# A hybrid attention layer on one core: TensorE's order in the attention stages written out as a fixed software pipeline

## The chip, the cores and the metric

The kernel runs on one core of a Trainium2 chip. The metric is the device time of one execution in microseconds (us), as the median of several runs. A trace of one further, profiled execution is there for reading: the busy spans of the engines, their waits, and the transfers.

## The reference

One layer of a decoder works on one sequence of 2048 tokens with 1024 channels, all in float32. Eight heads of width 64 use forgetting attention (FoX), eight others stick-breaking attention; all are causal.

```python
h = rms_norm(x, g_attn) * (1.0 + scale_a) + shift_a     # shift, scale, gate: silu(c) @ w_ada + b_ada
q_f, k_f, v_f, q_s, k_s, v_s, f_logit = split(h @ w_in)
# FoX:            F = cumsum(log_sigmoid(f_logit + b));  softmax(q.k / 8 + F[t] - F[s]) over s <= t, times v
# stick-breaking: A[t,s] = sigmoid(z_ts) * prod_{s<j<t} (1 - sigmoid(z_tj)) over s < t, times v;  z = q.k / 8
x = x + gate_a * (concat(head_rms_norm(o_fox), head_rms_norm(o_sb)) @ w_out)
h = rms_norm(x, g_mlp) * (1.0 + scale_m) + shift_m
u = causal_depthwise_conv(h @ w_up)                      # width 3
x = x + gate_m * ((silu(u_gate) * u_val) @ w_down)
return rms_norm(x, g_final)
```

## The kernel before, in words

**Units.** Attention is cut into 32 units, `("sb" or "fox", p, tb)`: a kind, one of four pairs of heads, and one of four blocks of 512 queries. All stick-breaking units come first, then all FoX units; within a kind the pairs follow each other, and within a pair the blocks. A unit has a projection and an attention.

**The projection** (`proj`, `finish_proj`, `accumulate`; `norm_proj` for the first pair, which also normalises x) makes Q, K and V of the unit's 512 tokens. Each operand is held as a float32r number and its remainder (`split`: ScalarE copies, VectorE or GpSimd subtracts), so every product takes three matmuls. The normalised input lies in DRAM as eight tiles of 0.5 MB (`hs`), which come back through SyncE into ten `hp` buffers. Q takes 24 matmuls of 512 columns, K the same, both into `ps_pj` banks; V is made in even pairs only, for two pairs at once, by 96 matmuls of 256 columns, and read back from DRAM in odd pairs. Q and K pass through DMAs to be laid out (`Q<-q` L293, `K<-q` L303). Q has two buffers, K five, V six.

**The attention** of a unit (`attend`) goes through four head blocks: two blocks of 256 queries by two heads. A head block's keys come in chunks of 512.

- In stick-breaking (`sb_head`), for each chunk, from the last to the first, and each of two 128-query rows: logits (two matmuls, L378 and L379, into one of two `ps_qk` banks); two sigmoids on ScalarE (`rw`, `a`, L415 and L416); a scan on VectorE that multiplies from right to left (L424, L427); a product on GpSimd that yields the weights `a` (L431).
- In FoX (`fox_head`), for each row and all its chunks: logits, on VectorE the sum with the bias `Fb` and a running minimum (L460), and one exponential of the row on ScalarE (`p`, L464).
- Then both kinds go through `weighted`, once per 256 keys: four transposes of 128 x 128 on TensorE into one of three `ps_pt` banks (L388), a copy on ScalarE (L392) and a subtraction on VectorE (L393) into one of three `at` buffers, and four matmuls with V that add into the only `ps_pv` bank (L397). I call one such call a group. A unit has 6, 14, 22 or 30 groups for tb = 0 to 3, a pair 72.

When a head block's groups are done, ScalarE and VectorE read `ps_pv` out (L518, L519) into `oT`; after two heads `head_var` squares it on GpSimd and puts off a small matmul (L497) by 13 ticks.

**What sets the order.** The program is traced in an order: `interleave` runs the attention of a unit and pulls, in proportion, the steps of the next unit's projection and, in FoX, of `late_mod` (the other modulation vectors). But that is a priority only. A scheduler with a timing model of its own places the instructions of every engine, and it may take a later matmul ahead of an earlier one that has to wait. Each engine then runs the fixed sequence that results.

**Places named below.** `forget_sums` (L229) turns the forget-gate logits into the cumulated sums F: transfers, three activations, a transfer, four scans. It runs at unit ("sb", 1, 0). From unit ("sb", 0, 3) on, `long_rows` keeps a whole row in one `rw` buffer (4 of them). Pools are closed and opened at ("sb", 0, 3) and ("fox", 0, 0). After the last unit come `first_out`, the output projection, the MLP and the final norm.

Of the kernel before, what the change touches and what calls it, by code (L numbers as in the profile page):

```python
# [8 lines left out]
F32 = mybir.dt.float32  # L9
# [7 lines left out]
P = 128  # L17
# [16 lines left out]
def kernel(ctx: ExitStack, tc: tile.TileContext, x, c, w_ada, b_ada, g_attn, w_in, b_fgate,  # L34
# [96 lines left out]
    def interleave(main, n, fillers):  # L131
        live = [[g, k, 0] for g, k, _ in fillers if g is not None]
        for i, _ in enumerate(main):
            tick()
            for e in live:
                while e[2] < (i + 1) * e[1] / n:
                    e[2] += 1
                    if next(e[0], StopIteration) is StopIteration:
                        e[2] = 1 << 30
        for g, _, whole in fillers:  # L140
            if g is not None and whole:
                drain(g)

# [85 lines left out]
    def forget_sums():  # L229
        z = sx.tile([NTB * NH, TB], F32, name="fz", tag="a", bufs=8)  # L230
        e = sx.tile([NTB * NH, TB], F32, name="fe", tag="a", bufs=8)
# [9 lines left out]
        for t in range(NTB):  # L241
            e = sx.tile([NH, TB], F32, name="fl", tag="a", bufs=8)
            z = sx.tile([NH, TB], F32, name="fc", tag="a", bufs=8)
# [39 lines left out]
    def finish_proj(kind, p, tb, aq, w, hts, res, ak=None):  # L283
        Q = sb.tile([P, 2, 2, TB], F32R, name="Q", bufs=2)
        K = sb.tile([P, 2, TB], F32R, name="K", bufs=5)
# [22 lines left out]
        else:  # L308
            V1 = sb.tile([P, 4, 2, P], F32R, name="V", bufs=6)
# [72 lines left out]
    def weighted(o, kts, blk, V, hl, first, last, diag):  # L382
        b = pt()
        at = sb.tile([P, 2, 2 * 2 * P], F32R, name="at", bufs=3)
        order = [(1, 0), (0, 0), (0, 1), (1, 1)]
        for i, (kk, qi) in enumerate(order):
            if not (diag and i == 0):
                nc.tensor.transpose(b[:, i * P:(i + 1) * P], blk(kts[kk], qi), ident)  # L388
        lo = P if diag else 0
        if diag:  # L390
            nc.gpsimd.memset(f(at[:, :, 0:P]), 0.0)
        nc.scalar.activation(at[:, 0, lo:], b[:, lo:], AF.Copy)  # L392
        nc.vector.tensor_sub(at[:, 1, lo:], b[:, lo:], f(at[:, 0, lo:]))  # L393
        for kk, kt in enumerate(kts):
            for w in range(2):
                rhs = at[:, w].rearrange("p (s q) -> p s q", q=P)[:, 0:4:3, :] if kk else at[:, w, P:3 * P]
                nc.tensor.matmul(o[:, 0:2 * P], V[kt // 4][:, kt % 4, hl, :], rhs,  # L397
                                 start=first and kk == 0 and w == 0, stop=last and kk == 1 and w == 1)

    def sb_head(j, qc, hl, Q, K, V, o):  # L400
        n = (2 * j + 2 + 3) // 4
        right = [None, None]
        whole = [sx.tile([P, S + 1], F32, name="rw", bufs=4) for _ in range(2)] if long_rows else None
        for ch in range(n - 1, -1, -1):
            last = ch == n - 1
            at = []
            for qi in range(2):
                need = min(512, (2 * j + qi + 1) * P - ch * 512)
                b = logits(max(need, 2 * P), slice((qc + qi) * P, (qc + qi + 1) * P), hl, Q, K[ch])
                if long_rows:  # L410
                    r = whole[qi][:, ch * 512:ch * 512 + need + 1]
                else:
                    r = sx.tile([P, 512 + 1], F32, name="r", bufs=7)
# [3 lines left out]
                if last:  # L417
                    nc.gpsimd.memset(r[:, need:need + 1], 0.0)
                elif not long_rows:
                    nc.gpsimd.tensor_copy(r[:, need:need + 1], right[qi][:, 0:1])  # L420
# [618 lines left out]
```

## Time and profile before

| what | value |
|---|---|
| median of 3 runs | 3159.3 us (3159.17 to 3167.24) |
| the profiled execution | 3161.0 us |
| its span, first to last instruction | 3159.2 us |
| TensorE, VectorE, ScalarE, GpSimd busy | 94%, 67%, 52%, 42% of the span |
| granted TensorE clock, mean | 0.982 |
| first logits / first FoX transposes / last weighted sum of attention | 70.8 / 932.6 / 1621.0 us from the start of the span |

The page gives shares of busy time; the stage rows give the same for stretches that I chose. A matmul's recorded time contains its latency, and matmuls overlap, so a run of them is read by the time between its first start and last end. A wait is put down to the instruction that released it last.

### The profile page before, as it was taken

The page shows a single profiled execution, that of the slowest core. Times are in us where ns is not written, and L with a number is a line of the kernel's source. Part 1 is how long each engine was busy: PE and PEld are TensorE (multiplying, and loading weights), DVE is VectorE, ACT ScalarE, POOL GpSimd, SP SyncE. Part 2 cuts the span into 40 slices and gives each one's busy share as a digit, 9 for nine tenths or more (in the row PEclk, how much of TensorE's full clock was granted, in tenths as well). Part 3 has the DMA queues.
Part 4 walks back from the last instruction along what each step waited for, and adds up shares of the span by engine and source line. Part 5 has one row for each costly group of instructions (what it writes and reads, how often), then busy time and mean ns, then how long its engine had stood idle before and what let it go on. Part 6 is the DMA issues. An engine that isn't in the chain of part 4 may idle for free. (4 is left out here: it accounts for less than half of the span.)

```text
span 3159.2 us, 46407 instructions
## 1 busy us (share of the span) xinstructions
PE 2964.1 (94%) x15934; PEld 2510.7 (79%) x15934; DVE 2129.2 (67%) x3422; ACT 1650.8 (52%) x3033; POOL 1316.8 (42%) x1459
## 2 busy tenths in 40 slices
PE   6889798998989999999999989999899998999998
PEld 5778597987878789888877778888678887888887
DVE  6776689877876776556843587777987776244353
ACT  5664667766766565566743444444444443343332
POOL 2673666657553242242212344444444442322321
PEclk8999899999999999999999999999999999999999
DMA  9547432565346695685547632222222223554552
GB/s 266 185 128 272 136 112 87 165 212 158 128 129 211 203 304 194 171 308 162 170 130 228 214 104 81 87 83 86 88 74 86 84 89 115 197 203 154 192 200 90
DMA packets 292940, 496.51 MB, mean 157 GB/s; under 512 B 29448, under 2 KB 177664, under 8 KB 291680
## 3 DMA queue, kind: packets, MB, share of 16 engines
q1 hardware_dynamic: 281072, 480.92, 47.9%
q10 hardware_dynamic: 11632, 12.63, 1.1%
q8 instruction: 126, 2.06, 0.3%
q14 instruction: 110, 0.90, 0.1%
HBM read 352.61 MB, written 90.51 MB: 140 GB/s over the span
## 5 line engine op out<-in xcount | busy, mean ns | idle before, releaser
L828 PE MATMUL ps_o<-oa,wu 128*128 128x512 f32 x2088 | 503.1, 392 | 13.2 <-DVE oa L45 8.2
L828 PEld LDWEIGHTS ps_o<-oa,wu 128*128 128x128 f32 x2088 | 390.7, 188 | 104.0 <-DVE oa L45 12.4
L393 DVE TENSOR_TENSOR at<-ps_pt,at 128x512 fp32r<-128x512 f32 (+1 forms) x576 | 361.9, 650 | 127.2 <-ACT at L392 125.0
L281 PE MATMUL ps_pj<-hp,w_qk 128*128 128x512 f32 x1512 | 415.5, 408 | 29.6 <-DMA hp<-hs 10.0
L397 PE MATMUL ps_pv<-at,V 128*128 128x256 f32 x2304 | 415.5, 297 | 26.4 <-ACT at L392 11.9
L392 ACT ACTIVATE at<-ps_pt 128x512 fp32r<-128x512 f32 (+1 forms) x576 | 313.5, 577 | 210.6 <-PE ps_pt L388 165.2
L431 POOL TENSOR_TENSOR a<-a,rw 128x512 f32<-128x512 f32 (+2 forms) x272 | 332.3, 1237 | 208.3 <-DVE rw L427 82.8
L397 PEld LDWEIGHTS ps_pv<-at,V 128*128 128x128 f32 x2304 | 333.6, 191 | 64.0 <-DVE at L393 20.6
L281 PEld LDWEIGHTS ps_pj<-hp,w_qk 128*128 128x128 f32 x1512 | 280.7, 194 | 87.3 <-DMA hp<-hs 12.4
L45 DVE TENSOR_TENSOR wd<-wdraw,wd 128x1024 fp32r<-128x1024 f32 x88 | 113.1, 1285 | 260.9 <-ACT wd L44 260.9
L45 POOL TENSOR_TENSOR g<-graw,g 128x512 fp32r<-128x512 f32 x84 | 142.8, 1702 | 325.1 <-ACT g L44 324.2
L378 PE MATMUL ps_qk<-K,Q 128*128 128x512 f32 (+2 forms) x640 | 260.8, 409 | 15.3 <-ACT a L416 5.0
L978 PE MATMUL ps_o<-wd,g 128*128 128x512 f32 x1040 | 250.5, 391 | 8.7 <-ACT g L44 8.7
L427 DVE TENSOR_TENSOR_SCAN rw<-rw 128x512 f32<-128x512 f32 x168 | 242.1, 1460 | 19.0 <-ACT rw L415 18.5
L828 PE MATMUL ps_t<-ob,wu 128*128 128x512 f32 x984 | 241.5, 390 | 0.0
L320 PE MATMUL ps_pj<-w_v,hp 128*128 128x256 f32 (+1 forms) x1536 | 235.0, 290 | 5.5 <-DVE zn L326 2.5
L978 PEld LDWEIGHTS ps_o<-wd,g 128*128 128x128 f32 x1040 | 196.1, 189 | 49.9 <-ACT g L44 9.1
L379 PE MATMUL ps_qk<-K,Q 128*128 128x512 f32 (+2 forms) x640 | 235.1, 369 | 0.0
L44 ACT ACTIVATE wu<-wuraw 128x512 fp32r<-128x512 f32 x214 | 133.0, 626 | 189.0 <-PE ps_o L828 123.1
L388 PE MATMUL ps_pt<-edge,a 128*128 128x128 f32 x1088 | 186.2, 279 | 42.9 <-POOL a L431 40.1
L320 PEld LDWEIGHTS ps_pj<-w_v,hp 128*128 128x128 f32 x1536 | 210.3, 191 | 15.3 <-issue 3.1
L828 PEld LDWEIGHTS ps_t<-ob,wu 128*128 128x128 f32 x984 | 184.9, 188 | 38.9 <-ACT hf_m L733 0.3
(222 smaller groups left out, 5737.9 us busy)
## 6 DMA issues: line engine op xcount, KB each, us to landing
hp<-hs SPq DMA_DIRECT2D x224, 512.0 KB
wuraw<-in_w_up_dram SPq DMA_DIRECT2D x84, 512.0 KB
wdraw<-in_w_down_dram SPq DMA_DIRECT2D x84, 512.0 KB
Q<-q SPq DMA_DIRECT2D x128, 256.0 KB
g<-u SPq DMA_DIRECT2D x42, 512.0 KB
graw<-g SPq DMA_DIRECT2D x84, 256.0 KB
hs<-hp SPq DMA_DIRECT2D x32, 512.0 KB
K<-q SPq DMA_DIRECT2D x128, 128.0 KB
```

The costliest lines, as they stand in the source:

```text
L45: (lo_engine or nc.gpsimd).tensor_sub(lo, src, f(hi))
L281: nc.tensor.matmul(acc, w[kt][:, a, n], h[:, bb], start=kt == 0 and i == 0, stop=kt == KT - 1 and i == 2)
L320: nc.tensor.matmul(av[:, t * width:(t + 1) * width], hts[kt][:, a, tok], w[1][kt][:, bb, 0:width], start=kt == 0 and m == 0, stop=kt == KT ...
L378: nc.tensor.matmul(b[:, :cw], Q[:, hl, 0, qcols], K[:, hl, :cw], start=True, stop=False)
L379: nc.tensor.matmul(b[:, :cw], Q[:, hl, 1, qcols], K[:, hl, :cw], start=False, stop=True)
L392: nc.scalar.activation(at[:, 0, lo:], b[:, lo:], AF.Copy)
L393: nc.vector.tensor_sub(at[:, 1, lo:], b[:, lo:], f(at[:, 0, lo:]))
L397: nc.tensor.matmul(o[:, 0:2 * P], V[kt // 4][:, kt % 4, hl, :], rhs, start=first and kk == 0 and w == 0, stop=last and kk == 1 and w == 1)
L427: nc.vector.tensor_tensor_scan(rev, rev, rev, r[:, need:need + 1], ALU.mult, ALU.bypass)
L431: nc.gpsimd.tensor_mul(a[:, :need], a[:, :need], r[:, 1:need + 1])
L828: nc.tensor.matmul(b, w[:, p, j], o[:, q], start=first and i == 0, stop=last and i == 2, skip_group_check=True)
L978: nc.tensor.matmul(banks[t][n], g[:, a, t * P:(t + 1) * P], w[:, b, n * TB:(n + 1) * TB], start=k == 0 and i == 0, stop=k == NKD - 1 and i ...
```

## The change

Within the attention, a block `tc.manual_schedule(engines={PE})` makes TensorE take its instructions in the order in which the program is traced; the other engines are still placed by the scheduler. The traced order is now this.

- A work item is one chunk of a head block in stick-breaking (two parts, one per row, and up to two groups) and a whole head block in FoX (a part per row and chunk). `attend` keeps a queue of the current item and up to `reach` = 2 further ones (1 for units 0 to 2), whose `space` sums to at most 4; a FoX item of more than two chunks counts 2.
- For each group of the current item: its transposes with copy and subtraction (`turn`), then some parts (logits and what follows them) of the items ahead, then the sums (`add`) of the group that was turned two groups before.
- After each group, `fill_proj` makes some steps of projections. A step is six Q or K matmuls or twelve of V; a unit's generator has 18 steps in even pairs and 10 in odd ones, of which 16 and 8 have matmuls. In stick-breaking from unit 3 on, the steps are spread evenly over the groups of a pair, and reach up to two units ahead. In FoX, the next unit's steps are spread over the first 80% of the unit's groups, and what is missing is made at once when an item of the next unit is pulled into the queue.
- Units 0, 1 and 2 are run by an `attend` of their own each; units 3 to 15 share one, and units 16 to 31 another. Unit 0's projection is complete before its attention begins.
- Buffers: `rw` 4 to 3, `a` 8 to 7, `sq` 2 to 1; a new pool `ex` with one more Q, K and V while units 3 to 15 run. FoX rows of at most 1024 keys share one `p` buffer by two. The small matmul of `head_var` is put off by 4 ticks, not 13.

```diff
-    def interleave(main, n, fillers):
...
+        more = 3 < i < 16
+        Q = ex.tile([P, 2, 2, TB], F32R, name="Q") if more and i % 3 == 2 else sb.tile([P, 2, 2, TB], F32R, name="Q", bufs=2)
+        K = ex.tile([P, 2, TB], F32R, name="K") if i in (5, 13) else sb.tile([P, 2, TB], F32R, name="K", bufs=5)
...
+        def add(self):
+            head, at = self.head, self.at
+            if self.first:
+                head.o = pv()
...
+            if last:
+                head.right = getattr(head, "right", [None, None])
+                if long_rows:
+                    head.right[qi] = sx.tile([P, S + 1], F32, name="rw", bufs=3)
...
+            deferred.append([reduce, 4])
+
+    def attend(unit_list, behind, reach):
+        source = ((u, item, list(item.parts)) for u in unit_list for item in u.items())
+        queue = []
+        waiting = []
+        def room():
+            while len(queue) <= reach and sum(e[1].space for e in queue) < 4:
+                nxt = next(source, None)
+                if nxt is None:
+                    break
+                queue.append(nxt)
+            return [e[2] for k, e in enumerate(queue) if k and sum(x[1].space for x in queue[:k + 1]) <= 4]
+        def forward(n):
+            for parts in room():
+                while parts and n > 0:
+                    parts.pop(0)()
+                    n -= 1
+        room()
+        while queue:
+            unit, item, parts = queue[0]
+            while parts:
+                parts.pop(0)()
+            owed = sum(len(parts) for parts in room())
+            spread = max(1, -(-2 * len(item.groups) // 3))
+            for gi, g in enumerate(item.groups):
+                g.turn()
+                forward(-(-owed * (gi + 1) // spread) - (owed - sum(len(parts) for parts in room())))
+                if len(waiting) >= behind:
+                    waiting.pop(0).add()
+                waiting.append(g)
+                tick()
+                yield unit
+            queue.pop(0)
+            room()
+        while waiting:
+            waiting.pop(0).add()
+            yield unit
...
+    def enter_unit(u):
+        while made[0] <= u.index:
+            taken_before = taken[0]
+            fill_proj(taken_before + 1)
...
+    with tc.manual_schedule(engines={mybir.EngineType.PE}):
+        while not made[0]:
+            fill_proj(taken[0] + 1)
...
+        for u in plan[:3]:
+            first = taken[0]
+            for k, _ in enumerate(attend([u], 2, 1)):
+                fill_proj(first + (k + 1) * 24 // u.count, u.index + 2)
+            while made[0] <= u.index + 1:
+                fill_proj(taken[0] + 1)
...
+        for u in attend(plan[3:16], 2, 2):
+            seen[u.p] = seen.get(u.p, 0) + 1
+            if u.index == 4 and u.p == 1 and seen[1] == 1:
+                forget_sums()
+            fill_proj(base + sum(amount(p) for p in range(u.p)) + amount(u.p) * min(1, seen[u.p] / total[u.p]))
...
+        for u in attend(plan[16:], 2, 2):
+            seen[u.index] = seen.get(u.index, 0) + 1
+            share = seen[u.index] / u.count
+            fill_proj(base + sum(steps_of(i) for i in range(17, u.index + 1)) + steps_of(u.index + 1) * min(1, share / 0.8))
```

More of the change, by code (lines that the diff above doesn't have):

```diff
@@ L380, in logits @@
         return b
[L382 to L398, printed above, removed]
@@ L436, in sb_head, with __init__ @@
+    class SbItem:
+        def __init__(self, head, ch):
+            self.head, self.ch, self.space = head, ch, 1
+            self.at = [None, None]
+            head_last = ch == head.n - 1
+            nk = min(4, 2 * head.j + 2 - 4 * ch)
+            self.parts = [lambda qi=qi: self.weights(qi) for qi in range(2)]
+            self.groups = []
             for m in range(0, nk, 2):
                 kts = [4 * ch + m, 4 * ch + m + 1]
[L438 to L439 removed]
```

354 lines of the change are left out of this document (202 added, 152 removed).

## The prediction

> **What bounds the kernel now.** I read the page's head, then the busy time of the engines by stage, then TensorE's waits. The stage rows have these columns: stretch, its length, busy time and instructions of TensorE (PE), its weight loads (PEld), VectorE (DVE), ScalarE (ACT) and GpSimd (POOL), granted clock, DMA share, GB/s.
>
> ```profile
> span 3159.2 us, 46407 instructions
> ...
> PE 2964.1 (94%) x15934; PEld 2510.7 (79%) x15934; DVE 2129.2 (67%) x3422; ACT 1650.8 (52%) x3033; POOL 1316.8 (42%) x1459
> ...
> 81.50:250.30 168.80, 146.18 (x920) 126.48 (x919) 123.02 (x172) 103.64 (x221) 113.89 (x134) 0.95 0.48 157
> 250.30:917.30 667.00, 600.27 (x3865) 526.72 (x3865) 529.84 (x663) 438.45 (x946) 414.52 (x494) 0.98 0.49 152
> 917.30:1621.00 703.70, 673.35 (x4378) 595.06 (x4376) 465.57 (x1343) 423.06 (x783) 210.62 (x346) 0.99 0.65 206
> ```
>
> TensorE is the busiest engine (94%), so its idle time is what a new order can win back: 22.6 us while units 0 to 2 of stick-breaking run (81 to 250), 66.7 us in the rest of stick-breaking (to 917), 30.4 us in FoX (to 1621). The code behind 1621 is untouched.
>
> Matmuls overlap, so busy time hides slack, and I recount the stage from 250 to 917 by issue spacing. Three long unbroken runs of one kind of matmul, from the timeline, and then that stage's groups (count, then busy us and mean ns of one):
>
> ```profile
> 1652.10 10.49 PE L641 MATMUL ps_o<-wo,mix 128*128 128x512 f32 x45
> 1609.72 1.47 PE L388 MATMUL ps_pt<-edge,p 128*128 128x128 f32 x12
> 1608.40 1.48 PE L397 MATMUL ps_pv<-at,V 128*128 128x256 f32 x11
> ...
> L281 PE MATMUL ps_pj<-hp,w_qk 128*128 128x512 f32 x699 | 188.5, 405 | 13.8 <-DVE q L45 9.8 <-DMA hp<-hs 2.7 <-DVE q L290 0.7
> L397 PE MATMUL ps_pv<-at,V 128*128 128x256 f32 x983 | 175.4, 295 | 7.2 <-ACT at L392 3.3 <-DVE at L393 2.3 <-DVE oT L519 1.5
> L388 PE MATMUL ps_pt<-edge,a 128*128 128x128 f32 x932 | 159.1, 277 | 40.5 <-POOL a L431 38.5 <-POOL rw L418 1.6 <-DVE var L505 0.3
> ...
> L378 PE MATMUL ps_qk<-K,Q 128*128 128x512 f32 (+2 forms) x272 | 109.7, 405 | 3.0 <-ACT a L416 2.9
> L379 PE MATMUL ps_qk<-K,Q 128*128 128x512 f32 (+2 forms) x273 | 100.7, 371 | 0.0
> ...
> L320 PE MATMUL ps_pj<-w_v,hp 128*128 128x256 f32 (+1 forms) x601 | 95.1, 287 | 2.3 <-DVE q L45 1.4 <-POOL w_v L45 0.9
> ```
>
> A run lasts one mean duration plus a spacing for each further matmul. So 512 columns cost 0.229 us ((10.49 - 0.405) / 44), a 128-column transpose 0.108 (1.19 / 11), 256 columns 0.118 (1.18 / 10). The stage needs 699 x 0.229 + 983 x 0.118 + 932 x 0.108 + 545 x 0.20 (seven logit matmuls in ten have 512 columns, the others 256 or 384) + 601 x 0.118 = 160 + 116 + 101 + 109 + 71 = 557 us, with some 10 us of small ones 567. Of 667 us, 100 are lost. The same ratio of need to busy, 567 / 600.3, makes FoX's need 636 of 704, its loss 68. (The Trainium skill, Perfetto Trace Analysis, section Identifying the Most-Contended Engine, calls matmul busy share a poor measure of the distance to the roofline. These rows agree: by busy time alone the two losses would be 67 and 30, not 100 and 68.)
>
> What is it lost to? TensorE's waits in the whole span (us in total, times, longest), and smaller stretches of stick-breaking:
>
> ```profile
> PE ps_pt L388 <- POOL a L431: 40.1, 46, 1.5
> PE ps_pv L397 <- ACT at L392: 11.9, 11, 2.5
> PE ps_pj L281 <- DMA hp<-hs: 10.0, 6, 2.9
> ...
> PE ps_pv L397 <- DVE oT L519: 4.4, 3, 3.0
> ```
>
> ```profile
> 346.50:388.20 41.70, 26.74 (x122) 21.00 (x120) 23.18 (x32) 24.49 (x57) 23.67 (x34) 0.75 0.74 215
> ...
> 476.30:543.50 67.20, 54.22 (x372) 46.66 (x371) 63.00 (x73) 48.89 (x103) 48.63 (x50) 1.00 0.32 99
> 543.50:660.60 117.10, 116.58 (x787) 105.83 (x786) 91.87 (x124) 77.67 (x174) 72.20 (x95) 1.00 0.56 173
> ...
> 851.40:917.30 65.90, 53.08 (x359) 45.35 (x358) 60.04 (x69) 46.59 (x94) 44.45 (x41) 1.00 0.30 94
> ```
>
> First, to transposes (L388) that reach TensorE before GpSimd has made the weights which they turn: 46 waits of at most 1.5 us. Second, to unevenness: 476 to 543 and 851 to 917 are last-block units (tb=3), nearly all attention, where DVE is busy 94% and 91% of the time and TensorE idles 13 us each time; at 543 to 660 TensorE is full (116.6 of 117.1) and DVE only 78%. Third, at 346 TensorE idles 15 us beside the forget-gate sums.
>
> **The change part by part.** Each engine has as many instructions in the changed program as in the old one, and SyncE as many DMAs: all of it is order and buffers. No row shows the new waits, so each is bounded.
>
> *Logits ahead.* A group's step costs TensorE four transposes, 0.43 us, a logit pair, 0.46, and four sums, 0.47: 1.36, and its share of projection. Logits now stand two items, four steps, ahead of their transposes: 5.4 us or more. Between them lie
>
> ```profile
> L415 ACT ACTIVATE rw<-ps_qk 128x512 f32<-128x512 f32 (+2 forms) x272 | 148.2, 545 | 51.1 <-PE ps_qk L379 49.3
> L392 ACT ACTIVATE at<-ps_pt 128x512 fp32r<-128x512 f32 (+1 forms) x246 | 137.0, 585 | 79.0 <-PE ps_pt L388 49.3 <-PE ps_pv L397 14.4 <-POOL a L431 7.5
> ...
> L427 DVE TENSOR_TENSOR_SCAN rw<-rw 128x512 f32<-128x512 f32 x168 | 242.1, 1460 | 19.0 <-ACT rw L415 18.5
> L431 POOL TENSOR_TENSOR a<-a,rw 128x512 f32<-128x512 f32 (+2 forms) x272 | 332.3, 1237 | 208.3 <-DVE rw L427 82.8 <-DVE rw L424 46.6 <-ACT a L416 27.6
> ...
> L393 DVE TENSOR_TENSOR at<-ps_pt,at 128x512 fp32r<-128x512 f32 (+1 forms) x246 | 152.7, 647 | 39.6 <-ACT at L392 38.7
> ```
>
> a sigmoid, a scan and a product, 0.55 + 1.46 + 1.24 = 3.3 us: covered, with 2 us to spare, so most of the 40 us goes. If DVE's queue runs over a step late, the cover is gone and the transposes wait as today.
>
> *Sums two groups behind.* Copy and subtraction take 0.59 + 0.65 = 1.2 us, 2.7 behind a scan; two steps are 2.7. Just covered: most of the 11.9 us goes.
>
> *Projections even.* They are dealt out over a pair's 72 groups: in pairs 1 and 2, 56 steps that cost TensorE 6 x 0.229 = 1.37 us each, so 1.07 per group. TensorE then needs 2.4 us per group, DVE 0.65 + 1.46 = 2.1: TensorE is the later engine all through, and the 13 us holes fill. DVE comes next: 529.8 us of work in the stage, 564 at its best rate of 94%, against TensorE's 567. That near parity is why I don't take the whole loss back. Between the 0.4% that the full stretch idles and the 15% of today (100 of 667) I allow 4% over the need, near the full stretch, whose mix the new order spreads: 590 us.
>
> *Forget sums.* DMA, three activations, DMA, scans, in order as before:
>
> ```profile
> 355.14 0.68 DVE L238 SCALAR_TENSOR_TENSOR fe<-fz,fe 32x512 f32<-32x512 f32 x1 [7.13 <-ACT fe L237]
> ...
> 359.40 1.21 DVE L245 TENSOR_TENSOR_SCAN fc<-fl 8x512 f32<-8x512 f32 x1 [2.94 <-DMA fl<-log_f]
> ```
>
> DVE's queue stands 7.1 and 2.9 us for them, and attention with it. Of the 15 us I keep 12. Where pools change, the pipeline drains and fills with no other work: 5 us here. Stage: 590 + 12 + 5 = 607, **60 less**; bounds 10 and 85.
>
> *FoX.* An item is a head's whole rows, one or two ahead. Projections stay one unit ahead, the rest of one made in a burst when the next unit's items are pulled. 636 x 1.04 = 661, and 10 at its first head, which has only its bias loads to wait for: 671, **32 less**. A burst needs eight hp tiles of 0.5 MB, 20 us at this stage's 206 GB/s, beside 5.5 us of Q matmuls: if none of that is hidden, four bursts lose 58, so the bounds are -26 and 55. I take the near end, as 224 such loads cost 10.0 us of waits today.
>
> *Units 0 to 2* are attended one by one, so each pays a fill (3.3) and a drain (2.7), 18 us, and the norm's transposes and products stand in fixed order too. That is the size of today's 22.6 idle us: 0, bounds 25 worse and 15 better. *Unit 0's V* comes wholly ahead of the first logits, 48 matmuls of it formerly behind:
>
> ```profile
> 70.81 0.58 PE L378 MATMUL ps_qk<-K,Q 128*128 128x256 f32 x1 [3.44 <-DMA K<-q]
> ...
> 71.84 6.98 PE L320 MATMUL ps_pj<-w_v,hp 128*128 128x264 f32 x48
> ```
>
> 7.0 us later, less the 3.4 that hid nothing; 0, at worst 4.
>
> *Buffers.* rw goes from 4 to 3, a to 7, sq from 2 to 1. At a head's start the second row waits for a product issued three steps earlier, 4 us or more for a chain of 3.3: 0 (otherwise see the second rival). One more Q, K and V free SyncE's queue, which waits for Q's old readers and holds the hp loads behind it:
>
> ```profile
> SPq L293 <- PE ps_qk L379: 113.2, 13, 34.5
> ```
>
> TensorE sees that only in its 10.0 us of waits on hp; I count it within the 4%.
>
> **Sum.** The profiled execution took 3161.0 us (its span is 3159.2), 1.7 over the median of the runs, 3159.3, and inside their 3159.2 to 3167.2. 3161 - 60 - 32 = 3069; as a median **3067**.
>
> **The rivals.** *DVE paces it.* With TensorE fed evenly DVE still reaches only 85% (today 79% over the stage): 530 / 0.85 = 623, + 17 = 640, 27 less; with FoX's 32, **3100**. For it: the 94% was reached where DVE alone was late. Against: its input is now further ahead.
>
> *Buffers, not order.* The 46 like gaps (40 us) come from too few rows in flight, and there are now fewer. Then only the holes between units close, 60 - 40 = 20, and half of FoX's 32: **3123**. Against: the releaser that the row names is a product, not a freed buffer, and POOL idles 208 us before it, mostly for scans. (The Trainium skill, Perfetto Trace Analysis, section Optimization Strategy, holds that one gap repeated on the engine that should be full can mean too few buffers. By that rule this rival is right.)
>
> *It does nothing:* the data are late, whatever the order: **3159**.
>
> *Slower, at the head switch.* There is one ps_pv bank: a head's first sum must wait until ACT and DVE have read out the last head's.
>
> ```profile
> L519 DVE TENSOR_TENSOR oT<-ps_pv,o 64x256 f32<-64x256 f32 x52 | 21.5, 414 | 22.3 <-ACT o L518 21.3
> L518 ACT ACTIVATE o<-ps_pv 64x256 f32<-64x256 f32 x52 | 19.8, 382 | 33.1 <-PE ps_pv L397 32.6
> ```
>
> 0.38 + 0.41, behind a sigmoid and a scan 2.8 us, against 0.9 (transposes and logits) or 2.3 (and a projection step) between the two sums. All of TensorE's work now queues behind that sum. A stall of 0.5 to 1.9, mean 1.2, at 128 heads is 154 us: 3067 + 154 = **3221**; the change loses from 0.7 us per head on. Against: such waits are 4.4 us today, and while TensorE waits DVE works off its queue, so only the time in which TensorE is the later engine is lost.
>
> *Full:* 1.5% over the need, 576 + 17 and 646 + 5: 74 and 53 less, 3032, and **3020** with a gain in units 0 to 2.
>
> **How the numbers follow.** Forecast, 3040 to 3092: 0.47. DVE paces, 3093 to 3112: 0.17. Buffers, 3113 to 3149: 0.10. Nothing, 3150 to 3169: 0.04. Slower: 0.12. Full, under 3040: 0.10. A measurement of this kernel tells about 0.3% from no change, so: faster 0.84, same 0.04, slower 0.12. The range, 3010 to 3165, leaves out the slower case and little else.
>
> **What would show it.** Right: the stage to 917 some 60 us shorter, DVE near 90% in early and late units alike, a-transposes waiting under 10 us on POOL. Wrong: waits of first sums on oT over 50 us in all (head switch); DVE at 85% while TensorE idles (DVE paces); the waits on POOL unchanged (buffers); units 0 to 2 longer than 194 us, or TensorE waiting on hp for tens of us in FoX.

## The result and the profile after

| | before | after |
|---|---|---|
| median, runs on the same chip | 3163.3 us (4 runs) | 3373.8 us (4 runs, 3359.7 to 3383.3) |
| ratio, 95% interval | | 1.066 (1.0615 to 1.0705) |
| the profiled execution, its span | 3161.0, 3159.2 us | 3371.3, 3369.5 us |
| granted clock, mean | 0.982 | 0.957 |

The changed kernel is 6.6% slower, where 2.9% faster was forecast. The page's head and the stages of the changed kernel, cut at the same places of the program as before (first groups, end of unit 2, end of unit 15, end of attention):

```profile
span 3369.5 us, 46393 instructions
...
PE 3024.5 (90%) x15934; PEld 2550.1 (76%) x15934; DVE 2155.2 (64%) x3422; ACT 1666.0 (49%) x3033; POOL 1279.0 (38%) x1459
...
81.10:304.30 223.20, 164.54 (x951) 139.61 (x950) 116.84 (x177) 109.57 (x228) 96.04 (x137) 0.86 0.36 119
304.30:998.20 693.90, 593.81 (x3679) 518.31 (x3677) 547.20 (x655) 433.59 (x937) 386.12 (x495) 0.94 0.44 135
998.20:1829.60 831.40, 726.83 (x4542) 632.91 (x4543) 475.16 (x1349) 435.68 (x788) 209.26 (x346) 0.95 0.58 184
```

Units 0 to 2 take 54 us more, units 3 to 15 27 more, FoX 128 more, and what follows attention 2. Three things are in that.

**TensorE stands still longer.** Length less busy time is 58.7, 100.1 and 104.6 us, against 22.6, 66.7 and 30.4: 144 us more. Its waits, by stage (us in total, times, longest):

```profile
PE ps_pt L383 <- POOL a L471: 37.1, 21, 6.3
PE ps_pj L268 <- POOL hp L45: 10.3, 11, 2.4
PE ps_pj L268 <- ACT hp L44: 6.0, 7, 1.9
...
PE ps_pv L398 <- DVE oT L422: 59.0, 36, 4.2
PE ps_qk L368 <- ACT a L458: 19.6, 3, 19.0
PE ps_pt L383 <- POOL a L471: 11.6, 12, 1.8
...
PE ps_pv L398 <- DVE oT L422: 23.5, 25, 2.1
PE ps_pj L268 <- DMA hp<-hs: 21.6, 6, 12.6
PE ps_pt L383 <- ACT p L515: 16.7, 18, 3.5
PE ps_qk L368 <- DVE mn L510: 16.6, 20, 3.3
PE ps_qk L368 <- DMA K<-q: 11.2, 2, 9.2
```

Each stage has another wait on top: in units 0 to 2 transposes on GpSimd's product, in units 3 to 15 a head's first sum on the read-out of the last head (L422 is the addition into `oT`), in FoX five kinds of 11 to 24 us.

**TensorE runs at half rate more often.** In the trace's clock records every stretch is at 1.0 or 0.5. Within attention there are 33 half-rate stretches, 225 us, against 10 and 55 us before; TensorE was busy in 162 us of them, against 40. Q and K matmuls that follow each other start every 0.43 us there and every 0.229 outside, so about half of that time is lost: some 60 us more. With the 144 this is 204 of the 210.

**Work has moved.** The groups of units 3 to 15 (count, then busy us and mean ns):

```profile
L268 PE MATMUL ps_pj<-hp,w_qk 128*128 128x512 f32 x624 | 171.1, 412 | 0.0
...
L310 PE MATMUL ps_pj<-w_v,hp 128*128 128x256 f32 (+1 forms) x485 | 66.9, 293 | 0.0
```

Before there were 699 and 601. By the prediction's spacings (75 x 0.229 + 116 x 0.118) that is 31 us of projections less. FoX has some 28 us of them, which the scheduler used to pull ahead of it (75 of the first kind and 96 of the second), units 0 to 2 the rest. So units 3 to 15 lost 27 us with 31 us less to do, and of FoX's 128, 28 are no loss.

**One head switch, read from the timeline** (start, us, instruction; in brackets the idle time before it):

```profile
497.71 0.34 PE L369 MATMUL ps_qk<-K,Q 128*128 128x384 f32 x1
...
498.95 0.59 ACT L457 ACTIVATE rw<-ps_qk 128x512 f32<-128x512 f32 x1
499.43 0.60 ACT L458 ACTIVATE a<-ps_qk 128x512 f32<-128x512 f32 x1
499.57 2.20 DVE L466 TENSOR_TENSOR_SCAN rw<-rw 128x512 f32<-128x512 f32 x1
...
500.05 0.38 ACT L421 ACTIVATE o<-ps_pv 64x256 f32<-64x256 f32 x1
...
501.81 0.42 DVE L422 TENSOR_TENSOR oT<-ps_pv,o 64x256 f32<-64x256 f32 x1
...
502.28 1.01 PE L398 MATMUL ps_pv<-at,V 128*128 128x256 f32 x3 [4.22 <-DVE oT L422]
```

TensorE's last logits end at 498.05. ACT's half of the read-out (L421) goes at 500.05, behind two sigmoids, and DVE's (L422) at 501.81, behind a scan that TensorE's own lookahead had put into the queue. The next sum starts when that is done, 4.22 us later, and nothing else may go ahead of it. The same place in windows (TensorE's busy time is the second figure, the granted clock the third from the end):

```profile
493.30:496.70 3.40, 3.40 (x22) 2.92 (x21) 2.49 (x3) 2.45 (x7) 3.40 (x4) 1.00 0.32 79
496.70:500.10 3.40, 1.35 (x11) 1.03 (x9) 2.50 (x4) 2.67 (x7) 3.40 (x5) 1.00 0.92 221
500.10:503.50 3.40, 1.22 (x5) 1.22 (x6) 3.34 (x4) 1.69 (x4) 3.40 (x5) 0.50 0.97 235
503.50:506.90 3.40, 3.40 (x12) 2.71 (x11) 0.70 (x1) 0.00 (x0) 1.96 (x3) 0.50 0.15 39
506.90:510.30 3.40, 3.40 (x22) 2.92 (x21) 1.89 (x2) 2.19 (x5) 0.66 (x1) 0.99 0.00 0
```

A window in which TensorE was busy for 1.35 of 3.4 us is followed by 6.8 us at 0.50, half of them with TensorE full.

### The profile page after: what moved, and what is told of

Its sections match the earlier page's. It is cut to its first block, busy times and chain, and to the rows that moved or that the text cites. A ratio compares the mean times of both kernels' runs of the same rounds, so it can differ in the third digit from the quotient of the medians.

```text
span 3369.5 us, 46393 instructions
## 1 busy us (share of the span) xinstructions
PE 3024.5 (90%) x15934; PEld 2550.1 (76%) x15934; DVE 2155.2 (64%) x3422; ACT 1666.0 (49%) x3033; POOL 1279.0 (38%) x1459
## 4 chain that ended last, share of the span: by engine, by line
PE 41%; DMA 8%; DVE 8%; POOL 4%; issue 4%; ACT 3%; SPq 1%; POOLq 0%; DVEq 0%; ACTq 0%
PE ps_o L969 8%; PE ps_o L1119 7%; PE ps_t L1119 4%; PE ps_pj L268 3%; PE ps_bc L1119 3%; PE ps_t L969 3%; PE ps_pv L398 3%; PE ps_pt L383 2%; PE ps_o L734 2%; PE ps_pj L310 2%; DMA wuraw<-in_w_up_dram 2%; DVE wu L45 2%; PE ps_qk L368 1%; PE ps_qk L369 1%; DMA hp<-in_w_ada_dram 1%
## 5 line engine op out<-in xcount | busy, mean ns | idle before, releaser
L387 ACT ACTIVATE at<-ps_pt 128x512 fp32r<-128x512 f32 (+1 forms) x576 | 328.8, 574 | 379.8 <-PE ps_pt L383 339.5
L388 DVE TENSOR_TENSOR at<-ps_pt,at 128x512 fp32r<-128x512 f32 (+1 forms) x576 | 375.4, 654 | 212.2 <-ACT at L387 208.5
L398 PE MATMUL ps_pv<-at,V 128*128 128x256 f32 x2304 | 399.8, 296 | 86.4 <-DVE oT L422 82.6
L398 PEld LDWEIGHTS ps_pv<-at,V 128*128 128x128 f32 x2304 | 348.5, 197 | 139.2 <-DVE oT L422 106.4
L268 PE MATMUL ps_pj<-hp,w_qk 128*128 128x512 f32 x1512 | 417.5, 413 | 39.3 <-DMA hp<-hs 21.6
L471 POOL TENSOR_TENSOR a<-a,rw 128x512 f32<-128x512 f32 (+2 forms) x272 | 302.5, 1118 | 268.9 <-DVE rw L466 95.1
L368 PE MATMUL ps_qk<-K,Q 128*128 128x512 f32 (+2 forms) x640 | 290.2, 454 | 56.7 <-ACT a L458 19.6
L45 DVE TENSOR_TENSOR wd<-wdraw,wd 128x1024 fp32r<-128x1024 f32 x88 | 112.6, 1280 | 262.6 <-ACT wd L44 262.6
L45 POOL TENSOR_TENSOR g<-graw,g 128x512 fp32r<-128x512 f32 x84 | 145.1, 1730 | 323.5 <-ACT g L44 320.4
L466 DVE TENSOR_TENSOR_SCAN rw<-rw 128x512 f32<-128x512 f32 x168 | 260.8, 1559 | 6.5 <-ACT rw L457 6.3
L369 PE MATMUL ps_qk<-K,Q 128*128 128x512 f32 (+2 forms) x640 | 243.5, 382 | 0.0
L383 PE MATMUL ps_pt<-edge,a 128*128 128x128 f32 x1088 | 183.5, 285 | 56.5 <-POOL a L471 51.2
L310 PE MATMUL ps_pj<-w_v,hp 128*128 128x256 f32 (+1 forms) x1536 | 204.8, 289 | 3.1 <-ACT w_v L44 1.8
L383 PEld LDWEIGHTS ps_pt<-edge,a 128*128 128x128 f32 x1088 | 136.8, 147 | 86.4 <-POOL a L471 61.6
```

The lines of the kernel that those rows point to most:

```text
L45: (lo_engine or nc.gpsimd).tensor_sub(lo, src, f(hi))
L268: nc.tensor.matmul(acc, w[kt][:, a, n], h[:, bb], start=kt == 0 and i == 0, stop=kt == KT - 1 and i == 2)
L310: nc.tensor.matmul(av[:, t * width:(t + 1) * width], hts[kt][:, a, tok], w[1][kt][:, bb, 0:width], start=kt == 0 and m == 0, stop=kt == KT ...
L368: nc.tensor.matmul(b[:, :cw], Q[:, hl, 0, qcols], K[:, hl, :cw], start=True, stop=False)
L369: nc.tensor.matmul(b[:, :cw], Q[:, hl, 1, qcols], K[:, hl, :cw], start=False, stop=True)
L383: nc.tensor.transpose(b[:, i * P:(i + 1) * P], self.blk(self.kts[kk], qi), ident)
```

## The experiments

Theory B, formed from these views: the *fixed order as such* costs the time, since any wait of any matmul is now everyone's. Theory A: the head switch on the one bank, the prediction's slower rival. Theory C: not the holding to the order, but the order that the program traces, and the buffers. Lengths of the stages are taken from the first to the last subtraction of the groups (L388); intervals are for the ratio to the kernel before, which took 3161.6 to 3162.4 us beside these runs. A stage's length comes from one trace: in the six traces in which units 3 to 15 are fixed and not otherwise changed, they take 680 to 694 us.

| run | median us | ratio (95%) | units 0-2 | 3-15 | FoX |
|---|---|---|---|---|---|
| before | 3162 | | 169 | 667 | 703 |
| after | 3374 | 1.066 (1.0615 to 1.0705) | 223 | 694 | 831 |
| e1_free_order | 3156.3 | 0.998 (0.997 to 0.9991) | 174 | 661 | 696 |
| e4_fixed_sb | 3267.5 | 1.0331 (1.0313 to 1.0348) | 226 | 694 | 726 |
| e5_fixed_3to15 | 3210.4 | 1.0151 (1.0128 to 1.0174) | 174 | 689 | 723 |
| e18_fixed_fox | 3274.3 | 1.0352 (1.0329 to 1.0375) | 174 | 648 | 829 |
| e2_two_pv | 3318.9 | 1.0503 (1.0484 to 1.0521) | 228 | 646 | 823 |
| e3_act_release | 3316.9 | 1.0498 (1.0481 to 1.0516) | 225 | 650 | 821 |
| e9_mid_two_pv | 3202.0 | 1.0124 (1.0106 to 1.0143) | 176 | 644 | 759 |
| e6_before_two_pv | 3237.6 | 1.0238 (1.022 to 1.0256) | 172 | 688 | 748 |
| e10_mid_act | 3180.3 | 1.0061 (1.0043 to 1.0079) | 172 | 650 | 729 |
| e7_reach1 | 3369.5 | 1.0662 (1.0641 to 1.0683) | 227 | 684 | 835 |
| e11_first_units | 3348.8 | 1.0589 (1.0574 to 1.0603) | 205 | 688 | 828 |
| e12_warm | 3381.3 | 1.0688 (1.0669 to 1.0707) | 241 | 680 | 826 |
| e14_attention_fixed | 3284.4 | 1.038 (1.0361 to 1.0399) | 194 | 718 | 749 |
| e17_attention_act | 3269.5 | 1.0335 (1.0311 to 1.0359) | 196 | 713 | 742 |
| e19_attention_act_first | 3253.9 | 1.0284 (1.0264 to 1.0304) | 175 | 706 | 744 |

### Is it the fixed order?

**e1_free_order**

```diff
-    with tc.manual_schedule(engines={mybir.EngineType.PE}):
+    with ExitStack():
```

> The changed kernel with one thing undone: TensorE's instructions are no longer held in the order in which the program issues them, so a matmul that is ready may go ahead of one that waits. The lookahead of two items, the sums two groups behind, the even projections and all buffers stay. Theory B (the fixed order as such costs the time: whatever wait a matmul has, everything behind it waits too): most of the 210 us come back and the logits' gain of about 27 us (wait on the POOL product 38.5 to 11.6 us in units 3 to 15) remains, 3120 to 3170 us. Theory A (the head switch on the one bank of the sums): the bank is as single as before, but other work fills the wait, so also a return, though only of the 82.6 us on the read-out and of the half-rate time behind them: 3230 to 3290 us. Theory C (the order in which the program issues the work, and the smaller buffers, are at fault, not the holding to it): 3340 to 3390 us.

Measured 3156.3 us: theory B; A and C fall as causes of the whole. The stages of this run:

```profile
82.10:255.80 173.70, 149.81 (x936) 129.96 (x937) 124.81 (x176) 103.88 (x223) 116.18 (x136) 0.94 0.47 156
255.80:916.60 660.80, 602.43 (x3848) 529.65 (x3847) 540.90 (x660) 439.94 (x944) 398.77 (x494) 0.98 0.49 153
916.60:1612.50 695.90, 670.81 (x4365) 592.30 (x4364) 464.01 (x1340) 425.20 (x782) 211.36 (x346) 0.99 0.65 208
```

All 210 us are back, the clock too (0.94, 0.98, 0.99), with the new traced order and buffers. But the lookahead's gain is gone as well: the transposes wait again.

```profile
PE ps_pt L383 <- POOL a L471: 38.0, 36, 3.0
```

**e4_fixed_sb, e5_fixed_3to15, e18_fixed_fox**: the fixed order in some stages only (here and below, the comments beside the lines are not part of the code).

```diff
+    order = ExitStack()
+    order.enter_context(tc.manual_schedule(engines={mybir.EngineType.PE}))   # e4: at unit 0; e5: at unit 3; e18: at unit 16
...
+        order.close()        # e4 and e5: behind unit 15; e18: behind unit 31
```

> The changed kernel with TensorE's order fixed only through units 0 to 15; in the FoX half (units 16 to 31) a ready matmul may go ahead again. Theory B: the FoX stage, 831 us against 704 before, returns to 680 to 720 us, the time to 3225 to 3265 us, units 0 to 15 unchanged at 223 + 694 us. Theory A: only the 23.5 us of head-switch waits that lie in FoX and some half-rate time come back, 3320 to 3350 us. Theory C (program order, buffers and the projection bursts of the two-item lookahead): FoX stays above 800 us, 3350 to 3380 us.

> The changed kernel with TensorE's order fixed for units 3 to 15 alone; units 0 to 2 and the FoX half are free. If the stages add up (free order took 173.7, 660.8 and 695.9 us for units 0 to 2, 3 to 15 and FoX; the fixed order took 693.9 for units 3 to 15), the time is 3156 + 33 = 3189 us, 3175 to 3205, and the wait of first sums on the read-out stays near 59 us there. If what a fixed stage loses depends on what the stage before it leaves over, it would be outside that.

> The changed kernel with TensorE's order fixed in the FoX half alone, units 0 to 15 free. Fully fixed, FoX took 831 us with 670 us of issue time in it; free, 696 with 641, so 28 us of projections are only moved there by the fixed stage before. If FoX's own fixed order costs the other 107 us, FoX takes 795 to 810 us here and the time is 3255 to 3270 us. If most of the loss was handed over by the fixed stages before it, FoX is below 760 us and the time below 3220.

Each stage is slow where its order is fixed and only there: units 0 to 2 take 223 to 226 us fixed, 174 free; FoX 829 to 831 fixed, 723 to 726 free behind a fixed stage and 696 behind a free one. e5 and e4 came out 5 and 2 us above their expectations and e18 4, most likely for one reason: some 28 us of projections stay on FoX's side of the border as soon as either side is fixed (720, 720 and 714 Q and K matmuls in FoX, 646 in e1). The two FoX stages, of e4 and of e18, and units 3 to 15 of e18:

```profile
1000.20:1725.90 725.70, 699.66 (x4528) 619.59 (x4529) 468.13 (x1346) 429.55 (x788) 211.82 (x346) 0.99 0.65 210
```

```profile
255.00:902.80 647.80, 578.38 (x3688) 503.50 (x3687) 536.41 (x654) 436.84 (x937) 405.80 (x494) 0.98 0.47 147
902.80:1731.50 828.70, 724.56 (x4536) 631.53 (x4534) 475.18 (x1349) 436.15 (x788) 208.97 (x346) 0.95 0.59 183
```

For the same work, then, the fixed order costs FoX 829 - 726 = 103 us and units 3 to 15 694 - 648 = 46 us (32 by the shortest of the six traces), not the 33 by which they are longer than in e1.

### The head switch

**e2_two_pv** and **e3_act_release**, in the fully fixed order:

```diff
-    pt = lambda: bank(psb, "pt", 3)      # e2
-    pv = lambda: bank(psb, "pv", 1)
+    pt = lambda: bank(psb, "pt", 2)
+    pv = lambda: bank(psb, "pv", 2)
...
+            nc.scalar.activation(o1, o[0:HD, 0:2 * P], AF.Copy)      # e3: then oT = o1 + o2 from SBUF, o1 and o2 one buffer each
```

> The changed kernel with two banks for the sums and two, not three, for the transposes; the fixed order stays. Theory A (head switch): the 82.6 us in which first sums wait for the read-out fall below 10, and with them part of the half-rate time behind these gaps (291 us at half rate against 117.7 before): 3240 to 3300 us, the stages of units 3 to 15 (59.0 us of that wait) and FoX (23.5 us) gaining most, units 0 to 2 nothing. Theory B (the fixed order as such): the wait goes but the next one in line (transposes on the second bank's copy and subtraction, the softmax's exp and the weights' DMA in FoX) takes its place, 3320 to 3380 us. A loss beyond 3390 us would say that the third bank for the transposes was worth more than the second for the sums.

> The changed kernel with the bank of the sums read out by two copies on ACT, the addition on DVE then reading two SBUF tiles; one small ACT copy more per head (128 of about 0.4 us) and DVE is no longer on the way to the bank's release. If the head-switch wait is DVE's queue (the profile names the addition on DVE as what ends it), the 82.6 us fall to about a third and the time to 3290 to 3330 us. If what the first sum waits for is equally late on ACT (sigmoids queue there), the wait stays at 60 us or more under ACT's name and the time is 3360 to 3400 us.

Both take 55 to 57 us off, nearly all in units 3 to 15 (646 and 650 against 694), so the 59.0 us there were real, and they hung on DVE's scan queue, as e3 shows. In that stage the two runs take as long as e18 needs for the same work in free order: as far as single traces tell, the head switch is all that its fixed order cost. Their rows for units 3 to 15, e2 and then e3:

```profile
310.40:955.90 645.50, 574.86 (x3679) 504.78 (x3677) 556.77 (x654) 432.31 (x937) 391.45 (x495) 0.97 0.47 145
305.30:954.90 649.60, 576.92 (x3678) 501.75 (x3677) 569.12 (x654) 448.98 (x989) 406.46 (x495) 0.97 0.46 143
```

What they leave in the whole span, in e2 and then in e3:

```profile
PE ps_pt L383 <- POOL a L471: 62.5, 45, 6.6
PE ps_pt L383 <- DVE at L388: 25.9, 40, 2.6
```

```profile
PE ps_pv L398 <- ACT o L423: 28.1, 39, 2.6
PE ps_pt L383 <- POOL a L473: 63.5, 45, 5.9
```

With two banks the wait is gone and the transposes wait more, 25.9 us of it for the third bank that was taken from them (3.7 before that). e2 lies between the two theories, 19 us over A's range and 1 below B's; e3 is inside its first range. Theory A holds for a quarter of the loss. Whether the addition could simply be put ahead of the scan in DVE's queue was not tried.

**e9_mid_two_pv**, **e6_before_two_pv**, **e10_mid_act**: e5's edit with e2's; e2's edit on the kernel before; e5's with e3's from unit 3 on.

> As the run with the order fixed for units 3 to 15 alone, and with two banks for the sums and two for the transposes. With two banks the fixed order took 645.5 us for units 3 to 15, less than the free order (660.8) or the kernel before (667.0): theory A (the fixed lookahead is good for the stick-breaking stage, and only the single bank spoils it) gives 3156 - 15 = 3141 us, 3130 to 3155, faster than both kernels. The rival: the free stages need the third bank for the transposes more than a second one for the sums, and give the 15 us back, 3150 to 3180 us.

> The kernel before with two banks for the sums and two for the transposes, nothing else: the control for the bank split. In a free order the scheduler already fills the head switch (first sums waited 4.4 us on the read-out there), so theory A expects no gain from it: 3155 to 3185 us. A gain of over 10 us would say that the second bank is worth something whatever the order.

> The changed kernel with TensorE's order fixed for units 3 to 15 alone, three banks for the transposes everywhere, and, in units 3 to 15 alone, the single bank of the sums read out by ACT (two copies a head). The run with that fixed stage and nothing else took 173.6, 689.1 and 723.2 us for the stages; the fully fixed run with ACT's read-out took 649.6 us in units 3 to 15. If these add up: 3210 - 39 = 3171 us, 3155 to 3180, that is within 0.6% of the kernel before: the fixed lookahead is worth some 11 us against the free order inside its stage, and the FoX half, which takes over less finished work from a fixed stage (723 us against 696), eats it. If FoX falls back to 696 us behind a faster stage, 3140 to 3150 us.

The bank split was misjudged in free stages, by both theories: the kernel before loses 75 us by it, and e9's FoX 36 against e5's. The waits of the sums on subtraction and copy in e6, and the first of them in the kernel before, suggest that the third bank is what lets a free scheduler turn a group ahead:

```profile
PE ps_pv L397 <- DVE at L393: 65.3, 94, 1.8
PE ps_pv L397 <- ACT at L392: 25.1, 28, 2.5
...
PE ps_pv L397 <- DVE at L393: 8.9, 20, 1.1
```

e10 is the best that a fixed stage gave here, 0.6% slower than before: 650 us in units 3 to 15, level with e18's 648 for the same work in free order. Its edit reaches further than its expectation says: the condition `if long_rows` stays true in FoX, where the trace has 64 of the added copies, so its FoX (729 us, 723 in e5) is not e5's unchanged.

### Bursts, the first units, and the clock

**e7_reach1**: `attend(plan[16:], 2, 1)` in FoX, for `(plan[16:], 2, 2)`.

> The changed kernel, fully fixed, with the FoX half looking one item ahead, not two. A unit has four items; with two ahead the first item of the next unit is fetched when the third of this one starts, and what is missing of its projections is issued at once, in one run: after 2 of 6 groups in the short units. With one ahead it is fetched a quarter of a unit later. If these bursts are what starves DVE and TensorE in FoX (short units of 47.2, 39.7, 31.8 and 34.0 us against 34.4, 13.0, 19.5 and 13.2 before; hp waits 21.6 us), FoX falls from 831 to 780 to 815 us and the time to 3325 to 3360 us. If the projections of a unit of 6 groups are too much for it however they are spread, or the softmax chain now gets too little lead (waits on the exp and on the minimum above 40 us), the time is 3365 to 3420 us.

The second case: 3369.5 us, FoX 835. The waits on hp halve, and those on the exponential double:

```profile
PE ps_pt L383 <- ACT p L515: 36.3, 28, 4.8
...
PE ps_pj L268 <- DMA hp<-hs: 10.9, 5, 8.8
```

**e11_first_units**

```diff
-        for u in plan[:3]:
-            first = taken[0]
-            for k, _ in enumerate(attend([u], 2, 1)):
...
+        for u in attend(plan[:3], 2, 2):
+            seen[u.index] = seen.get(u.index, 0) + 1
+            fill_proj(first.setdefault(u.index, taken[0]) + seen[u.index] * 24 // u.count, u.index + 2)
```

> The changed kernel, fully fixed, with units 0 to 2 run as one pipeline that looks two items ahead across their borders, in place of three that start empty and look one ahead; the projections' share of each unit is unchanged but the rest of it is no longer forced at the unit's end. Theory: in units 0 to 2 the lookahead is too short for the chain of sigmoid, scan and product (37.1 us of TensorE waits on the product there, the longest 6.3) and these gaps bring the half rate (clock 0.86): the waits fall to 15 us or less, the stage from 223 to 185 to 205 us, the time to 3335 to 3355 us. Rival: the norm chain of the projections paces the stage, and the forced rest only moves: 218 to 230 us, 3365 to 3385 us.

As the theory had it: the stage takes 205 us, the time falls by 25, and in the whole span the transposes' waits on the product fall from 51.2 us to

```profile
PE ps_pt L383 <- POOL a L471: 14.4, 14, 2.5
```

The edit changes three things at once (two items ahead, no stop at the borders, no forced rest), and the 18 of this stage's 54 us are theirs together. The rival has a part in what is left: waits of projections on the split of the normalised input (`hp`, L45 on GpSimd) went from 10.3 to 21.2 us.

**e12_warm**: in units 0 to 2, ahead of each group's transposes,

```diff
+                for _ in range(3):
+                    nc.tensor.matmul(b, self.head.Q[:, 0, 0, 0:P], self.head.K[0][:, 0], start=True, stop=True)
```

> The changed kernel with three matmuls of 512 columns more ahead of each group's transposes in units 0 to 2 (42 groups, 126 matmuls, 0.227 us each at the full clock: 29 us), their result overwritten by the transposes: work for nothing that TensorE does while the transposes wait for the product. Theory: the half rate there (clock 0.86, about 58 us of the stage) follows TensorE's idleness, so the granted clock of the stage rises to 0.92 or more, and the stage grows by less than half of the added work or not at all (215 to 235 us). Rival: the half rate has another cause (the kind of matmuls, DMA): the clock stays at 0.84 to 0.88 and the stage grows by 20 us or more, 243 us and over.

Inconclusive. The stage grew by 17 us for 29 us of idle work, and its clock rose from 0.86 to 0.88 only:

```profile
80.20:320.80 240.60, 193.62 (x1075) 161.38 (x1074) 116.37 (x177) 109.88 (x229) 96.48 (x137) 0.88 0.34 112
```

The added work is no cure, and a weak test: 47 of the stage's 59 idle us stayed. That the half rate follows idleness rests on the records of all runs (below), not on this one.

### Held projections, or a rigid attention?

**e14_attention_fixed**: `manual_schedule` replaced by a chain through the attention's matmuls alone; their sequence is that of the changed kernel, all else on TensorE is free.

```diff
+    def chained(op, *args, **kw):        # for logits, transposes of groups and sums
...
+            with tc.issue_after(chain[0]):
+                chain[0] = op(*args, **kw).ins
```

> The changed kernel with the order of the attention's matmuls (logits, transposes, sums) kept to the last one as the change issues it, and everything else on TensorE free: projections, norm transposes and the heads' variances may go wherever they are ready. Theory B1 (the projections are what a wait can be filled with, and holding them in place takes that filler away): the waits of the first sums and of the transposes are filled, at most a quarter of the 210 us stays, 3160 to 3215 us. Theory B2 (the fixed order of the attention itself costs the time: sums two groups behind and logits ahead in a rigid order that DVE, ACT and POOL cannot follow): 3300 to 3370 us.

Neither: 3284.4 us, 89 of the 210 us back. Its stages:

```profile
78.10:272.20 194.10, 168.42 (x1035) 146.01 (x1033) 121.48 (x183) 107.64 (x234) 102.41 (x137) 0.93 0.58 192
272.20:990.00 717.80, 613.79 (x3758) 546.58 (x3757) 555.25 (x655) 435.31 (x939) 371.06 (x494) 0.92 0.41 126
990.00:1739.20 749.20, 681.44 (x4379) 600.95 (x4378) 473.68 (x1342) 431.49 (x782) 210.88 (x346) 0.98 0.61 194
```

By stage the answer differs. FoX does the work of e1 in 749 us against 696: of its own 103 us about half belong to the held projections, half to the attention's order. Units 0 to 2 recover 29 of 54 us although they make 83 Q and K matmuls more, 19 us. Units 3 to 15 recover nothing (718, with 9 us more of projections than in the changed kernel): with all else free, first sums still wait there for the read-out, and transposes for the product. In the whole span:

```profile
PE ps_pv L373 <- DVE oT L431: 64.1, 40, 3.1
PE ps_pt L373 <- POOL a L480: 51.7, 37, 4.7
```

Of these, 46.9 and 36.6 us lie in units 3 to 15, against 59.0 and 11.6 in the changed kernel. The scheduler puts many of the free projections early in a pair, which leaves few for the last-block units; but that is not where the time goes: in ("sb", 1, 3) and ("sb", 2, 3) e1 has about as few (48 and 56 projection matmuls, 45 and 47 here) and takes 63 and 80 us, against 70 and 81. The run changes two things in units 3 to 15, the freedom and the place of the projections, and their shares stay open.

**e17_attention_act**: e14 with e3's read-out. **e19_attention_act_first**: that with e11's edit.

> As the run with the attention alone in fixed order, with the single bank of the sums read out by ACT. If the head switch stays a wait there that projections cannot fill, this gains what it gained in the fully fixed order, 40 to 60 us; if they fill it, under 10 us, or the extra 128 ACT copies cost up to 10.

> As the run with the attention alone in fixed order and ACT's read-out, with units 0 to 2 run as one pipeline two items ahead, which took 18 us off that stage in the fully fixed order. If projections already fill the waits on the product there, 0 to 5 us less than without it; if not, 10 to 20 us less. If the attention's order is worth what it was made for, this is the version that comes below the kernel before: 3120 to 3150 us; if not, 3160 us or more.

15 us for the read-out, between the two expectations, and 16 more for the first units (175 us, as free). Of the 20 us by which that stage falls, 17 are 73 Q and K matmuls that are now made in units 3 to 15, which take 7 us less all the same. 3253.9 us is still 2.8% over the kernel before. The only version that comes below both kernels is e1, the new traced order with free issue, by 0.2%.

## Why the prediction was wrong

- **The recount by issue spacing** (567 of 667 us): no run contradicts it, but the step from it to a gain failed. It took the 100 lost us as what an order can win. The changed order lost 158 (694 us for 567 - 31 = 536 of need), and the free one in e18 still 112 (648).
- **Logits ahead: right where it was worked out.** In units 3 to 15 the wait on the product fell from 38.5 to 11.6 us, 27 of the forecast "most of the 40". In units 0 to 2 it rose from 1.6 to 37.1, so in the whole span it grew, from 40.1 to 51.2.
- **Sums two groups behind: right in its own term.** The wait of sums on ACT's copy went from 11.9 to 0.8 us:

```profile
PE ps_pv L398 <- ACT at L387: 0.8, 2, 0.7
```

- **Projections even: the failed step in units 3 to 15.** "4% over the need" left no room for a wait that nothing may pass. What the runs showed in its place is the head switch: 59.0 us of waits, and 44 to 48 us of the stage's time come back when the read-out is relieved (e2, e3), all that the fixed order cost there (46, e18). Measured were 694 us for 607 forecast, with 31 us less to do; the term also missed that a fixed region does not pull FoX's projections in. That held projections are what leaves the wait unfilled is not shown: e14 frees them, and 46.9 us of it stay. (Of the 56 steps in the term, 48 have matmuls: 0.91 us per group, not 1.07. TensorE still comes out later than DVE.)
- **Forget sums:** 12 us forecast, one wait of 19.0 us measured, under the name of the sigmoids that stand behind them; TensorE could do nothing else in it.
- **FoX: the largest miss**, 831 us for 671. The burst is there as described, with its price: 42 Q and K matmuls with one group of attention between them, and then

```profile
1221.21 4.25 PE L268 MATMUL ps_pj<-hp,w_qk 128*128 128x512 f32 x18
...
1226.91 5.63 PE L268 MATMUL ps_pj<-hp,w_qk 128*128 128x512 f32 x24
...
1245.18 1.19 PE L268 MATMUL ps_pj<-hp,w_qk 128*128 128x512 f32 x2 [12.64 <-DMA hp<-hs]
```

  one wait of 12.64 us for a tile from DRAM. The term was valued at its near end because 224 loads cost 10.0 us "today"; but today other matmuls went ahead while a tile was on its way. That is the failed step: the price of a wait in a free order was carried into a fixed one. All of hp and K cost 32.8 us in FoX, not 58; the exponential and the minimum, which had no term at all, cost 33.3, and the read-out 23.5. Of the 128 us by which FoX grew, 28 are projections that came over, 74 are idle time and some 20 the half rate. How the 103 us of FoX's fixed order divide among these waits stays open: e7 took 11 us off the waits on hp and no time off the stage.
- **Units 0 to 2:** 0 forecast, 54 lost, beyond the bound of 25. The fills were named, but only once per unit; with one item of lookahead the transposes waited on the product 21 times, up to 6.3 us, and the half rate followed.
- **The rival at the head switch** had the mechanism and the place: 82.6 us on `oT`, over the 50 that it named. Its size was off: 61 waits of 1.35 us on average, not 128 of 1.2, and 55 us in the time (e2, e3), not 154. It named a quarter of the loss.
- **The other rivals.** In the changed kernel DVE is 79% busy in units 3 to 15 (547 of 694), not 85, and the gaps at the product did not persist there. But "DVE paces it" is not ruled out as what comes next: with the head switch relieved DVE is 86% and 88% busy and the stage takes 646 and 650 us (e2, e3), near that rival's 85% and 640.
- **The clock** had no term, and took some 60 us.

In short: the forecast priced the fixed order by the two waits that it removes and gave the others a flat 4%, or the little that they cost in the free order: 4.4 us for the read-out, 10.0 for the loads. In the fixed order these two were 82.6 and 21.6.

## What to carry to other kernels

Before an order is fixed by hand, list every kind of wait that the engine still has, with its number and length, and ask what each costs when nothing may pass it. A free order's small wait on a transfer or a read-out is not the price of that transfer; it is what the scheduler's filling has left of it. Fix the least that the gain needs, and look where a bank's release queues on another engine. That a partly fixed order can beat a free one was not shown here.

## What the runs showed of the hardware

The half rate comes sooner than long gaps. In the changed kernel, 24 of the 33 half-rate stretches in attention had no gap of 3.4 us between matmuls in the 6.8 us before them; what all 33 had was a last 3.4 us in which TensorE was idle for 47% or more (37% in the kernel before, whose ten stretches had no such gap at all). They last 3.4 us or a multiple of it, up to 20.5.

In every trace all changes of rate lie on one grid of 3.413 us. Cut into these windows, the attention of all 17 traces shows what comes after a window (number of windows, by the share of it in which TensorE was idle):

| rate in the window | idle | next at full rate | next at half rate |
|---|---|---|---|
| full | under 40% | 6852 | 3 |
| full | 40 to 60% | 242 | 161 |
| full | 60% or more | 0 | 259 |
| half | under 10% | 390 | 11 |
| half | 10 to 20% | 34 | 27 |
| half | 20% or more | 1 | 234 |

A window at full rate that was idle for half or more was followed by the half rate in 376 of 429 cases, and the full rate came back, but for one case, only after a window that was over 80% busy. This is an order in time, in every run; the one edit that aimed at it (e12) did not settle it.

The Trainium skill, TensorE: Matmul & The Clock Gate, section Part 1: The HAM clock gate (the "warmup" mystery), gives two states, half and full rate, and a free-running window of some 3.4 us; the records agree in both. Its condition for the half rate, one idle window, is stricter than these records if it means a window without any work: windows with half of their time busy were often enough. So idle time that comes in many waits of 1 to 3 us cost some 40% more than its length here (some 60 us beside 144).
